# Differential scores: the keys' low-part pass on 64 rows, the two maps' passes adjacent in opposite halves of the array's rows

## The chip, the cores and the metric

The kernel runs on one core of a Trainium2 chip. The metric is the device time of one execution in microseconds, the median of several runs; lower is better.

## The reference, cut to what matters

Two layers of a decoder trunk (sequence 1024, width 1024, float32) mix tokens in three ways: differential attention, a latent attention (MLA) and a sliding window. The change touches the first alone. It has 4 heads, and each head has two maps (m) of width 64 with a common value of width 128:

```
s = einsum('bqhmd,bkhmd->bhmqk', q, k) * 64 ** -0.5      # two maps per head
s = where(rel >= 0, s + bias[head], NEG)                       # causal; bias differs in the last 256 keys only
pm = softmax(s, axis=-1)
w = pm[:, :, 0] - lam * pm[:, :, 1]
o = einsum('bhqk,bkhe->bqhe', w, v)
```

## The kernel before, in words

**Precision.** Matmuls are done in fp32r. To come close to float32, an operand x is split into a high part H, x rounded (a cast on ScalarE, line 76), and a low part L = x - H (VectorE, line 91). A projection takes three products for each tile of 128 rows: HH, HL and LH (`group`, line 294).

**Scores of the differential attention.** A map is 64 wide, half of the 128 rows of TensorE's array. `stack_q` (line 453) stacks a query tile as qH in partitions 0 to 63 and qL in 64 to 127. `stack_k` (line 464) does the same for the keys, tile kA, and two DMAs for each map and half of the sequence make a second tile kB with the halves exchanged. So q.kA = qH.kH + qL.kL and q.kB = qH.kL + qL.kH, and two passes of 128 rows give all four products. `rows` (line 629) does this for one map of one query tile of 128 rows: `n = (i + 1) * 128` causal keys, in one chunk up to 512 and two chunks beyond (`chunks`, line 623). Each chunk takes a bank of PSUM with the tag "sc" (there are two), gets its two passes (`mm`, line 99), then the bias (line 762) and the maximum (line 639) on VectorE, and after the last chunk the exponentials on ScalarE (line 645), which free the banks.

**Order.** `da` (line 697) goes through 4 heads; a head has 4 blocks (`da_block`, line 751) of two query tiles. Of a tile, map 0 is written first, then one step of the block before (`late`, its transposes and products with V) and `FILL[2]` = 2 steps of filler, then map 1, the sum of the two maps, and again a step of `late` and `FILL[1]` = 2 steps. A filler is a projection that nobody waits for yet (the gates and the units of the next head); one step is 6 matmuls of 512 columns into one of three banks with the tag "mm". The order written is a priority only: the planner of the framework issues on each engine what is ready by its own estimate, so a matmul whose bank is not free yet lets later ones pass.

**The units of a head.** `prep` (line 710) returns the units for keys, queries and values; each loads 128 columns of the input weights, splits them, and multiplies them with the 8 pairs of tiles of hT, in two halves of the sequence.

```
# rows, lines 635-640: one chunk of one map
ps = self.psum("sc")
self.mm(ps[:, :w], [(q, k[:, k0:k0 + w]) for q, k in terms])     # terms: (q, kA), (q, kB)
near(ps, k0, w)
nc.vector.tensor_reduce(st[:, c:c + 1], ps[:, :w], AX.X, ALU.max, negate=len(ch) == 1)
```

The latent attention, which the change leaves alone, has one operation on 64 rows: at line 864 it transposes the values, which lie in partitions 64 to 127, four blocks of 64 by 128 at a time.

Of the kernel before, what the change touches and what calls it, by code (L numbers as in the profile page):

```python
# [10 lines left out]
F32 = mybir.dt.float32  # L11
F32R = mybir.dt.float32r
I32 = mybir.dt.int32
AF = mybir.ActivationFunctionType
ALU = mybir.AluOpType
AX = mybir.AxisListType

P = 128
S = 1024
D = 1024  # L20
DEPTH = 2
KT = D // P
# [5 lines left out]
FILL = (3, 2, 2, 1, 1, 5, 3)  # L28
BANKS = dict(mm=3, av=1, sc=2, tr=2)
OFF = dict(aq=0, ak=512, av=1024, az=1536, bq=2048, bkv=2304, bkr=2432, bz=2464,  # L30
           cq=2976, ck=3488, cv=3616, cz=3744, g=4256)
# [27 lines left out]
class Builder:  # L59
# [404 lines left out]
    def stack_k(self, pool, l, c, tiles, swapped):  # L464
# [8 lines left out]

        yield from self.unit(W, KT, self.hT, evac)

    def v_unit(self, pool, l, c, put):
        W = self.load_w(self.win(l, c))

        def evac(hf, ps):
            vT = pool.tile([P, 512], F32, tag="vT", bufs=1, name=self.uid("vT"))  # L480
            self.copy("a", vT, ps)
            tr = self.psum("tr")
            for t in range(4):
                self.nc.tensor.transpose(tr[:, t * P:(t + 1) * P], vT[:, t * P:(t + 1) * P], self.ident)
            put(hf, tr.rearrange("p (t d) -> p t d", t=4))

        yield from self.unit(W, KT, self.hT, evac)
# [141 lines left out]
    def rows(self, pl, n, terms, near, sums):  # L629
# [16 lines left out]
                                 accum_out=sums[:, c:c + 1])  # L646
        return e

    def weighted(self, pl, ws, b, vterms):

        nc = self.nc
        terms = []
        av = self.av = self.psum("av")
        self.square_sums(av)

        def add(last):
            for i, (w, x) in enumerate(terms):
                self.nc.tensor.matmul(av[:, 0:256], w, x, start=self.first and not i,  # L658
                            stop=last and i == len(terms) - 1)
            self.first = self.first and not terms  # L660
            terms.clear()

        self.first = True
        for kp in range(b + 1):
            tr = self.psum("tr")
            if kp == b:
                self.diag.reverse()
            H, L = self.diag[0] if kp == b else self.wt_tiles(pl)

            for a in range(2):  # L670
                kt = 2 * kp + 1 - a
                for q in range(2):
                    if kt <= 2 * b + q:
                        self.nc.tensor.transpose(tr[:, (2 * a + q) * P:(2 * a + q + 1) * P],  # L674
                                       ws[q][:, kt * P:(kt + 1) * P], self.ident)
            z = P if kp == b else 0
            self.split(H[:, z:], L[:, z:], tr[:, z:])
            add(False)
            for a in (1, 0):
                kt = 2 * kp + 1 - a  # L680
                terms += vterms(kt, H[:, a * 256:(a + 1) * 256], L[:, a * 256:(a + 1) * 256])
            yield
        add(True)
# [13 lines left out]
    def da(self, l):  # L697
        nc = self.nc
        v = self.vecs[l]
        with ExitStack() as ctx:  # L700
            pl = self.pool("da", ctx)
            bias = pl.tile([P, 4, 256], F32, name=self.uid("dab"))
            nc.sync.dma_start(bias, self.bias_ap(0, 4))
            heads = []
            self.diag_tiles(pl)
            s0 = pl.tile([P, 4, 8], F32, name=self.uid("s0"))
            ms = pl.tile([P, 4, 8], F32, name=self.uid("ms"))
            self.s0, self.ms = s0, ms

            def prep(h):  # L710
                t = {}
                for nm in ("q", "kA", "kB"):
                    t[nm] = [pl.tile([P, S], F32R, tag=f"{nm}{m}", bufs=2, name=self.uid(nm))
                             for m in range(2)]
                for nm in ("VH", "VL"):
                    t[nm] = pl.tile([P, 8, P], F32R, tag=nm, bufs=2, name=self.uid(nm))

                def put(hf, tr):
                    sl = slice(hf * 4, hf * 4 + 4)
                    self.split(t["VH"][:, sl], t["VL"][:, sl], tr)  # L720

                heads.append(t)
                return (self.stack_k(pl, l, OFF["ak"] + h * P, t["kA"], t["kB"]),
                        self.stack_q(pl, l, OFF["aq"] + h * P, t["q"]),
                        self.v_unit(pl, l, OFF["av"] + h * P, put))

            for g in prep(0):
                self.weave(g, 1)
            late = iter(())
            for h in range(4):  # L730
                nxt = []
                for b in range(4):
                    late = self.da_block(l, pl, h, b, heads[h], bias, late)
                    if not b and h < 3:
                        nxt = self.later(*prep(h + 1), front=True)
                self.drain(*nxt)
            self.weave(late, FILL[1])
            self.square_sums(self.psum("av"))

            f = lambda t: t.rearrange("p h i -> p (h i)")  # L740
            s0, ms = f(s0), f(ms)
            nc.vector.reciprocal(s0, s0)
            nc.vector.tensor_tensor(ms, ms, s0, ALU.mult)
            nc.vector.tensor_tensor(ms, ms, s0, ALU.mult)
            nc.scalar.activation(ms, ms, AF.Sqrt, bias=self.eps, scale=1.0 / P)
            nc.vector.reciprocal(ms, ms)
            nc.vector.tensor_tensor(ms, ms, s0, ALU.mult)
            self.put_rows(pl, l, "a", ms)
            self.fill(FILL[6])

    def da_block(self, l, pl, h, b, t, bias, late):
        nc = self.nc
        nlam = self.vecs[l]["nlam"]
        ws = []
        for i in (2 * b, 2 * b + 1):
            n = (i + 1) * P
            es = []

            def near(ps, k0, w):
                a = max(n - 256, k0)  # L760
                if a < k0 + w:
                    nc.vector.tensor_tensor(ps[:, a - k0:w], ps[:, a - k0:w],  # L762
                                            bias[:, h, a - n + 256:k0 + w - n + 256], ALU.add)

            sm = pl.tile([P, 6], F32, tag="sm", bufs=4, name=self.uid("sm"))
            for m in range(2):
                q = t["q"][m][:, i * P:(i + 1) * P]
                es.append(self.rows(pl, n, [(q, t["kA"][m]), (q, t["kB"][m])], near,
                                    sm[:, 2 * m:2 * m + 2]))
                if not m:  # L770
                    next(late, None)
                    self.fill(FILL[2])
            e0, e1 = es
            s0 = self.s0[:, h, i:i + 1]
            if n > 512:
                nc.vector.tensor_tensor(s0, sm[:, 0:1], sm[:, 1:2], ALU.add)
                nc.vector.tensor_tensor(sm[:, 2:3], sm[:, 2:3], sm[:, 3:4], ALU.add)
            else:
                nc.gpsimd.tensor_copy(s0, sm[:, 0:1])  # L779
            nc.vector.reciprocal(sm[:, 4:5], sm[:, 2:3])  # L780
            nc.vector.scalar_tensor_tensor(sm[:, 5:6], sm[:, 4:5], nlam, s0, ALU.mult, ALU.mult)
            nc.vector.scalar_tensor_tensor(  # L782
                e0[:, :n], e1[:, :n], sm[:, 5:6], e0[:, :n], ALU.mult, ALU.add)
            ws.append(e0)
            next(late, None)
            self.fill(FILL[1])
        self.weave(late, FILL[2])

        def vterms(kt, H, L):
            return [(t["VH"][:, kt], H), (t["VH"][:, kt], L), (t["VL"][:, kt], H)]  # L790

        def rest():
            yield from self.weighted(pl, ws, b, vterms)
            o = self.zp.tile([P, 256], F32, tag="o", bufs=2, name=self.uid("o"))
            av = self.av
            self.copy("a", o, av[:, :256])
            sq = pl.tile([P, 256], F32, tag="sq", bufs=2, name=self.uid("sq"))
            nc.scalar.activation(sq, av[:, :256], AF.Square)
            self.squares = sq, self.ms[:, h, 2 * b:2 * b + 2]
            nc.sync.dma_start(self.o_d[l, "a"][h * P:(h + 1) * P, b * 256:(b + 1) * 256], o)  # L800

        return rest()
# [398 lines left out]
```

## Time and profile before

| | us |
|---|---|
| median of 3 runs (2652.02 to 2655.14) | 2653.09 |
| the profiled execution | 2655.53 |
| its span, from the first to the last instruction | 2653.8 |
| TensorE busy | 2608.1 (98%) |
| VectorE busy | 1528.0 (58%) |
| ScalarE busy | 1240.5 (47%) |
| GpSimd busy | 389.4 (15%) |

Busy time is the union of an engine's instructions. A matmul's end is modelled, and matmuls overlap, so TensorE's pace is read from one start to the next.

### The profile page before, as it was taken

Reading aid. Unit: us, or ns where it says so; the run is one execution under the profiler, and the core shown is the slowest. Engines: PE = TensorE matmul, PEld = TensorE weight load, DVE = VectorE, ACT = ScalarE, POOL = GpSimd, SP = SyncE. Lnnn points to the kernel's source line nnn. Section 1 sums busy time; section 2 is a strip of 40 time slices with the busy share of each in tenths; the row PEclk is TensorE's granted clock in tenths of the full one; section 3 lists DMA queues with packets and bytes.
Section 4 is the critical chain, followed back from the end, with each engine's and each line's share of the span. In section 5 each row is a group of like instructions: output and inputs, shape, how many; then the busy total and the mean of one; then the engine's idle time right before and its main releaser. Section 6 shows DMA issues by size and latency. Waiting matters only on the chain.

```text
span 2653.8 us, 35805 instructions
## 1 busy us (share of the span) xinstructions
PE 2608.1 (98%) x13024; PEld 2148.4 (81%) x13024; DVE 1528.0 (58%) x2928; ACT 1240.5 (47%) x2695; POOL 389.4 (15%) x359
## 2 busy tenths in 40 slices
PE   8999999999999998999999999999999999989999
PEld 6788888888888876888877788888888888778877
DVE  5664767535666445655457637664366664456653
ACT  5553545435666433333445535554266664333332
POOL 2000000000000144134410000000000001440431
PEclk9999999999999999999999999999999999999999
DMA  6223222221112576353332322222211126754432
GB/s 193 60 70 103 59 64 63 70 74 51 46 45 59 166 240 199 119 181 114 118 88 62 89 82 64 62 63 66 65 47 50 46 66 211 237 174 138 143 116 96
DMA packets 296817, 269.21 MB, mean 101 GB/s; under 512 B 24272, under 2 KB 237456, under 8 KB 296512
## 3 DMA queue, kind: packets, MB, share of 16 engines
q1 hardware_dynamic: 295568, 262.19, 32.9%
q0 software_dynamic: 1072, 4.73, 0.6%
q8 instruction: 103, 1.69, 0.3%
q14 instruction: 74, 0.61, 0.1%
HBM read 194.93 MB, written 61.44 MB: 97 GB/s over the span
## 4 chain that ended last, share of the span: by engine, by line
PE 79%; DVE 7%; DMA 4%; issue 4%; ACT 3%; POOL 2%; SPq 1%; ACTq 0%; POOLq 0%; DVEq 0%
PE mm L303 56%; PE sc L102 8%; PE av L658 5%; PE tr L674 4%; DVE wL L91 2%; PE sc L303 1%; DMA sig<-g_d 1%; ACT wH L76 1%; PE tr L595 1%; DVE sig L1014 1%; POOL y L1016 1%; DMA wr<-w_ple_proj 1%; DVE y L1018 1%; POOL o L1045 1%; ACT big L76 1%
## 5 line engine op out<-in xcount | busy, mean ns | idle before, releaser
L303 PE MATMUL mm<-big,wH 128*128 128x512 f32 x4480 | 1447.8, 396 | 1.6 <-DVE big L91 1.1
L303 PEld LDWEIGHTS mm<-big,wH 128*128 128x128 f32 x4480 | 825.3, 188 | 149.5 <-DVE big L91 1.7
L303 PE MATMUL mm<-big,wL 128*128 128x512 f32 x2240 | 882.8, 394 | 4.1 <-DVE wL L91 3.9
L303 PEld LDWEIGHTS mm<-big,wL 128*128 128x128 f32 x2240 | 421.4, 188 | 86.6 <-DVE wL L91 6.6
L91 DVE TENSOR_TENSOR wL<-wr,wH 128x1024 fp32r<-128x1024 f32 (+2 forms) x268 | 274.9, 1034 | 300.7 <-ACT wH L76 299.0
L76 ACT CAST wH<-wr 128x1024 fp32r<-128x1024 f32 (+2 forms) x268 | 229.4, 863 | 274.2 <-PE mm L303 243.3
L645 ACT ACTIVATE e<-sc,st 128x512 f32<-128x512 f32 (+3 forms) x384 | 222.5, 583 | 123.2 <-DVE st L642 69.2
L639 DVE TENSOR_REDUCE st<-sc 128x1 f32<-128x512 f32 (+3 forms) x384 | 213.0, 555 | 89.8 <-PE sc L102 83.2
L76 ACT CAST wtH<-tr 128x512 fp32r<-128x512 f32 x204 | 116.5, 588 | 100.1 <-PE tr L674 81.7
L91 DVE TENSOR_TENSOR wtL<-tr,wtH 128x512 fp32r<-128x512 f32 x204 | 139.2, 684 | 38.7 <-ACT wtH L76 37.2
L674 PE MATMUL tr<-cm,e 128*128 128x128 f32 x864 | 148.4, 274 | 0.1
L76 ACT COPY zs<-mm 128x512 f32<-128x512 f32 x144 | 84.2, 584 | 104.1 <-PE mm L303 100.1
L674 PEld LDWEIGHTS tr<-cm,e 128*128 128x128 f32 x864 | 108.2, 142 | 17.9 <-DVE e L782 2.4
L102 PE MATMUL sc<-kA,q 128*128 128x256 f32 (+3 forms) x320 | 104.5, 336 | 1.5 <-ACT e L645 0.9
L91 POOL TENSOR_TENSOR kL<-vT,kH 64x512 fp32r<-64x512 f32 x32 | 42.0, 1312 | 426.3 <-ACT kH L76 357.4
L1041 POOL TENSOR_TENSOR sg<-sg,z 128x512 f32<-128x512 f32 x48 | 71.0, 1480 | 210.5 <-ACT sg L1040 198.6
L102 PE MATMUL sc<-kB,q 128*128 128x256 f32 (+3 forms) x320 | 98.8, 318 | 0.0
L1046 DVE TENSOR_TENSOR o<-o,sg 128x512 f32<-128x512 f32 x48 | 53.7, 1129 | 71.2 <-POOL o L1045 66.7
L762 DVE TENSOR_TENSOR sc<-sc,dab 128x256 f32<-128x256 f32 (+1 forms) x128 | 52.8, 413 | 65.6 <-PE sc L102 63.7
L1007 ACT ACTIVATE sig<-sig 128x1024 f32<-128x1024 f32 x48 | 50.9, 1060 | 79.2 <-DMA sig<-g_d 79.1
L779 POOL COPY s<-sm 128x1 f32<-128x1 f32 x32 | 6.3, 196 | 528.2 <-ACT e L645 528.2
L374 POOL TENSOR_TENSOR acc<-acc,sq 128x512 f32<-128x512 f32 x36 | 57.2, 1590 | 174.6 <-ACT sq L373 67.3
(295 smaller groups left out, 4163.0 us busy)
## 6 DMA issues: line engine op xcount, KB each, us to landing
wr<-w_in SPq DMA_DIRECT2D x108, 512.0 KB, 4.0
g_d<-zs SPq DMA_DIRECT2D x96, 256.0 KB, 2.1
sig<-g_d SPq DMA_DIRECT2D x48, 512.0 KB, 3.3
wr<-w_out SPq DMA_DIRECT2D x32, 512.0 KB, 4.6
wr<-w_ple_gate SPq DMA_DIRECT2D x32, 512.0 KB, 3.7
kB<-kA SPq DMA_DIRECT2D x80, 128.0 KB, 2.4
x<-x SPq DMA_DIRECT2D x16, 512.0 KB, 6.2
wr<-w_br_a SPq DMA_DIRECT2D x8, 512.0 KB, 5.1
```

The lines of the kernel that those rows point to most:

```text
L76: nc.scalar.copy(out, in_)
L91: (nc.vector if le == "v" else nc.gpsimd).tensor_tensor(L, src, h, ALU.subtract)
L102: self.nc.tensor.matmul(ps, w, x, start=i == 0, stop=i == n - 1)
L303: self.nc.tensor.matmul(ps, w, x, start=i == 0, stop=i == n - 1)
L374: (nc.gpsimd if eng == "g" else nc.vector).tensor_tensor(st, st, sq, ALU.add)
L639: nc.vector.tensor_reduce(st[:, c:c + 1], ps[:, :w], AX.X, ALU.max, negate=len(ch) == 1)
L645: nc.scalar.activation(e[:, k0:k0 + w], pss[c][:, :w], AF.Exp, bias=st[:, 0:1], accum_out=sums[:, c:c + 1])
L658: self.nc.tensor.matmul(av[:, 0:256], w, x, start=self.first and not i, stop=last and i == len(terms) - 1)
L674: self.nc.tensor.transpose(tr[:, (2 * a + q) * P:(2 * a + q + 1) * P], ws[q][:, kt * P:(kt + 1) * P], self.ident)
L762: nc.vector.tensor_tensor(ps[:, a - k0:w], ps[:, a - k0:w], bias[:, h, a - n + 256:k0 + w - n + 256], ALU.add)
L1041: nc.gpsimd.tensor_tensor(sg, sg, z, ALU.mult)
L1046: nc.vector.tensor_tensor(o, o, sg, ALU.mult)
```

## The change

The queries of map 1 are stacked the other way round (`rows_q`): qL in partitions 0 to 63, qH in 64 to 127. The keys' tile kA (`rows_k`) now holds the high part twice, in both halves, the second by one DMA; so the first pass, q.kA, is qH.kH + qL.kH. The low parts of both maps lie in one tile kL, map 0 in partitions 0 to 63, map 1 in 64 to 127. The second pass, qH.kL, takes 64 rows: rows 0 to 63 for map 0, rows 64 to 127 for map 1. The product qL.kL is no longer computed, and kB is gone.

`two_rows` takes the place of two calls of `rows`: `two` writes, for the first chunk of a tile, the 128-row passes of both maps into the two "sc" banks and then the two 64-row passes. Biases and maxima of both maps follow. A second chunk is done map by map, its 128-row and its 64-row pass one behind the other, in an "mm" bank. The first chunk is now up to 512 keys wide and the second gets the rest, at least 256. The steps of `late` and filler stand where they stood, after map 0's exponentials. The sliding window keeps `stack_k` and `stack_q`.

```diff
--- before.py
+++ after.py
@@ -470,6 +470,31 @@
                 self.split(tiles[m][0:64, sl], tiles[m][64:128, sl], ps[m * 64:m * 64 + 64])
                 self.nc.sync.dma_start(swapped[m][0:64, sl].bitcast(F32), tiles[m][64:128, sl].bitcast(F32))
                 self.nc.sync.dma_start(swapped[m][64:128, sl].bitcast(F32), tiles[m][0:64, sl].bitcast(F32))
+
+        yield from self.unit(W, KT, self.hT, evac)
+
+    def rows_q(self, pool, l, c, tiles):
+
+        W = self.load_w(self.win(l, c))
+
+        def evac(hf, ps):
+            sl = slice(hf * 512, hf * 512 + 512)
+            for m in range(2):
+                a, b = slice(m * 64, m * 64 + 64), slice(64 - m * 64, 128 - m * 64)
+                self.split(tiles[m][a, sl], tiles[m][b, sl], ps[a], scale=0.125)
+
+        yield from self.unit(W, KT, self.hT, evac)
+
+    def rows_k(self, pool, l, c, tiles, low):
+
+        W = self.load_w(self.win(l, c))
+
+        def evac(hf, ps):
+            sl = slice(hf * 512, hf * 512 + 512)
+            for m in range(2):
+                a, b = slice(m * 64, m * 64 + 64), slice(64 - m * 64, 128 - m * 64)
+                self.split(tiles[m][a, sl], low[a, sl], ps[a])
+                self.nc.sync.dma_start(tiles[m][b, sl].bitcast(F32), tiles[m][a, sl].bitcast(F32))
 
         yield from self.unit(W, KT, self.hT, evac)
 
@@ -646,6 +671,48 @@
                                  accum_out=sums[:, c:c + 1])
         return e
 
+    def two(self, pss, qs, ks, low, at=(0, 1)):
+
+        nc = self.nc
+        for ps, q, k in zip(pss, qs, ks):
+            nc.tensor.matmul(ps, q, k, start=True, stop=False)
+        for ps, q, m in zip(pss, qs, at):
+            a = slice(m * 64, m * 64 + 64)
+            nc.tensor.matmul(ps, q[a], low[a], start=False, stop=True)
+
+    def two_rows(self, pl, n, qs, kA, kL, near, sums):
+
+        nc = self.nc
+        ch = [(0, n)]
+        if n > 512:
+            b = max(n - 512, 256)
+            ch = [(0, n - b), (n - b, b)]
+        w = ch[0][1]
+        pss = [[self.psum("sc")] for _ in range(2)]
+        sts = [pl.tile([P, 2], F32, tag="st", bufs=8, name=self.uid("st")) for _ in range(2)]
+        self.two([p[0][:, :w] for p in pss], qs, [x[:, :w] for x in kA], kL[:, :w])
+        for m in range(2):
+            near(pss[m][0], 0, w)
+            nc.vector.tensor_reduce(sts[m][:, 0:1], pss[m][0][:, :w], AX.X, ALU.max, negate=len(ch) == 1)
+        for m in range(2):
+            st = sts[m]
+            if len(ch) == 2:
+                k0, w1 = ch[1]
+                ps = self.psum("mm")
+                a = slice(m * 64, m * 64 + 64)
+                self.mm(ps[:, :w1], [(qs[m], kA[m][:, k0:n]), (qs[m][a], kL[a, k0:n])])
+                near(ps, k0, w1)
+                nc.vector.tensor_reduce(st[:, 1:2], ps[:, :w1], AX.X, ALU.max)
+                nc.vector.tensor_reduce(st[:, 0:1], st[:, 0:2], AX.X, ALU.max, negate=True)
+                pss[m].append(ps)
+            e = pl.tile([P, S], F32, tag="e", bufs=4, name=self.uid("e"))
+            for c, (k0, w) in enumerate(ch):
+                nc.scalar.activation(e[:, k0:k0 + w], pss[m][c][:, :w], AF.Exp, bias=st[:, 0:1],
+                                     accum_out=sums[m][:, c:c + 1])
+            pss[m], ps, out = None, None, [e]
+            del e
+            yield out.pop()
+
     def weighted(self, pl, ws, b, vterms):
 
         nc = self.nc
@@ -709,9 +776,10 @@
 
             def prep(h):
                 t = {}
-                for nm in ("q", "kA", "kB"):
+                for nm in ("q", "kA"):
                     t[nm] = [pl.tile([P, S], F32R, tag=f"{nm}{m}", bufs=2, name=self.uid(nm))
                              for m in range(2)]
+                t["kL"] = pl.tile([P, S], F32R, tag="kL", bufs=2, name=self.uid("kL"))
                 for nm in ("VH", "VL"):
                     t[nm] = pl.tile([P, 8, P], F32R, tag=nm, bufs=2, name=self.uid(nm))
 
@@ -720,8 +788,8 @@
                     self.split(t["VH"][:, sl], t["VL"][:, sl], tr)
 
                 heads.append(t)
-                return (self.stack_k(pl, l, OFF["ak"] + h * P, t["kA"], t["kB"]),
-                        self.stack_q(pl, l, OFF["aq"] + h * P, t["q"]),
+                return (self.rows_k(pl, l, OFF["ak"] + h * P, t["kA"], t["kL"]),
+                        self.rows_q(pl, l, OFF["aq"] + h * P, t["q"]),
                         self.v_unit(pl, l, OFF["av"] + h * P, put))
 
             for g in prep(0):
@@ -763,13 +831,13 @@
                                             bias[:, h, a - n + 256:k0 + w - n + 256], ALU.add)
 
             sm = pl.tile([P, 6], F32, tag="sm", bufs=4, name=self.uid("sm"))
-            for m in range(2):
-                q = t["q"][m][:, i * P:(i + 1) * P]
-                es.append(self.rows(pl, n, [(q, t["kA"][m]), (q, t["kB"][m])], near,
-                                    sm[:, 2 * m:2 * m + 2]))
-                if not m:
-                    next(late, None)
-                    self.fill(FILL[2])
+            two = self.two_rows(pl, n, [x[:, i * P:(i + 1) * P] for x in t["q"]], t["kA"], t["kL"],
+                                near, [sm[:, 0:2], sm[:, 2:4]])
+            es.append(next(two))
+            next(late, None)
+            self.fill(FILL[2])
+            es.append(next(two))
+            two.close()
             e0, e1 = es
             s0 = self.s0[:, h, i:i + 1]
             if n > 512:
```

## Rows read from the trace of the kernel before

**Rows 1.** The page, engines over the span, and TensorE's granted clock in 40 slices.

```profile
PE 2608.1 (98%) x13024; PEld 2148.4 (81%) x13024; DVE 1528.0 (58%) x2928; ACT 1240.5 (47%) x2695; POOL 389.4 (15%) x359
...
PEclk9999999999999999999999999999999999999999
```

**Rows 2.** Busy time by stage: PE, PEld, DVE, ACT, POOL, clock, DMA share, GB/s.

```profile
252.00:507.00 255.00, 254.47 (x1343) 211.85 (x1343) 175.24 (x409) 126.58 (x317) 3.14 (x16) 1.00 0.24 66
```

**Rows 3.** What PE waited for from 252 to 507 us: total, times, longest.

```profile
PE sc L102 <- ACT e L645: 0.5, 2, 0.2
```

**Rows 4.** Timeline of PE: start, us, engine, line, operation, tiles, shapes, count.

```profile
256.24 0.28 PE L102 MATMUL sc<-kA,q 128*128 128x256 f32 x1
256.35 0.28 PE L102 MATMUL sc<-kB,q 128*128 128x256 f32 x1
256.47 0.40 PE L303 MATMUL mm<-big,wH 128*128 128x512 f32 x1
...
501.92 0.39 PE L102 MATMUL sc<-kA,q 128*128 128x512 f32 x1
502.15 0.39 PE L102 MATMUL sc<-kB,q 128*128 128x512 f32 x1
502.37 0.40 PE L303 MATMUL mm<-big,wH 128*128 128x512 f32 x1
502.60 0.39 PE L102 MATMUL sc<-kA,q 128*128 128x512 f32 x1
```

**Rows 5.** Line 102 from 252 to 507 us: count, ns min/median/max, first and last, shapes.

```profile
L102 PE MATMUL sc<-kA,q x95: 220/387/501, 254.6 to 506.4; 128*128 128x512 f32 x40, 128*128 128x256 f32 x24, 128*128 128x384 f32 x24, 128*128 128x128 f32 x7
```

**Rows 6.** Timeline around a group of 64-row transposes (L864), PE and its weight loads.

```profile
619.42 0.61 PE L303 MATMUL mm<-big,wH 128*128 128x512 f32 x2
...
619.88 0.19 PEld L303 LDWEIGHTS mm<-big,wH 128*128 128x128 f32 x1
620.10 0.39 PE L303 MATMUL mm<-big,wH 128*128 128x512 f32 x1
...
620.42 0.33 PEld L864 LDWEIGHTS tr<-cm,vT 64*128 64x128 f32 x4 [0.35 <-ACT vT L76]
620.42 0.46 PE L864 MATMUL tr<-cm,vT 64*128 64x64 f32 x4
620.81 0.19 PEld L303 LDWEIGHTS mm<-big,wH 128*128 128x128 f32 x1
620.81 0.50 PE L303 MATMUL mm<-big,wH 128*128 128x512 f32 x1
...
621.15 0.39 PE L303 MATMUL mm<-big,wL 128*128 128x512 f32 x1
```

**Rows 7.** Line 864, the 64-row transposes, whole span: count, ns min/median/max, shapes.

```profile
L864 PE MATMUL tr<-cm,vT x128: 221/223/273, 620.4 to 2161.5; 64*128 64x64 f32 x128
```

**Rows 8.** Timeline of PE around another group, between matmuls of 256 columns.

```profile
649.45 0.28 PE L658 MATMUL av<-wtH,vp 128*128 128x256 f32 x1
649.57 0.28 PE L658 MATMUL av<-wtL,vp 128*128 128x256 f32 x1
649.78 0.46 PE L864 MATMUL tr<-cm,vT 64*128 64x64 f32 x4
650.17 0.38 PE L658 MATMUL av<-wd,vp 128*128 128x256 f32 x1
```

**Rows 9.** Timeline of PE around four 128-row transposes.

```profile
882.23 0.39 PE L303 MATMUL mm<-big,wL 128*128 128x512 f32 x1
882.46 0.60 PE L674 MATMUL tr<-cm,e 128*128 128x128 f32 x4
882.81 0.71 PE L303 MATMUL mm<-big,wH 128*128 128x512 f32 x2
```

**Rows 10.** Instructions of tile kA, whole span: a cast and one swap DMA.

```profile
L76 ACT CAST kA<-mm x40: 571/582/586, 27.1 to 1733.2; 64x512 fp32r<-64x512 f32 x40
...
L471 SPq DMA_DIRECT2D kB<-kA x40: 461/462/1058, 32.8 to 1734.7; - x40
```

**Rows 11.** The page, groups by line: busy us, mean ns of one, idle before.

```profile
L645 ACT ACTIVATE e<-sc,st 128x512 f32<-128x512 f32 (+3 forms) x384 | 222.5, 583 | 123.2 <-DVE st L642 69.2
L639 DVE TENSOR_REDUCE st<-sc 128x1 f32<-128x512 f32 (+3 forms) x384 | 213.0, 555 | 89.8 <-PE sc L102 83.2
...
L674 PE MATMUL tr<-cm,e 128*128 128x128 f32 x864 | 148.4, 274 | 0.1
```

## The prediction

> **What bounds the kernel now.** I read the page first. TensorE is busy 98% of the span, VectorE 58%, ScalarE 47%, at a granted clock of nine tenths or more in all forty slices [rows 1]. Busy matmul time is modelled and overlaps, so I went on to the stage that is changed, the differential attention, which runs once in each of the two layers. In the first layer's, 255 us from 252 to 507 us, TensorE is busy 254.5 us and VectorE 175 [rows 2]. The waits of TensorE in it add up to 0.5 us, on ScalarE's exponentials that give score banks back [rows 3]. So nothing but TensorE's own instruction stream sets the length of this stage, because projection matmuls ("fillers") are put between the scores wherever they would wait. What the change does to the stream arrives in the total one to one; what it does to VectorE, ScalarE or the DMA queues hardly arrives at all.
>
> The stream is read from start to start. Scores of 512 columns follow each other, and other matmuls, every 0.227 us (501.92, 502.15, 502.37), 256 columns every 0.115 (256.24, 256.35, 256.47) [rows 4]; for 384 and 128 columns I take the same rate, 0.17 and 0.06. At that pace the weight loads cost nothing: each load starts about when the matmul ahead of its own starts, and is done before its own matmul (the load at 619.88 serves the matmul at 620.10) [rows 6].
>
> **Part 1, the number of matmuls and their columns: nothing.** Before, each chunk of each map is two passes of 128 rows. After, it is again two, the second on 64 rows. The first stretch has 95 records of the first pass [rows 5]; by the loops it is 4 heads x (4 tiles with one chunk + 4 with two, 12 chunks) x 2 maps = 96, and as many of the second. Columns per pass decide a matmul's time, and they stay; that half of the rows is idle shortens nothing by itself. The chunk order changes (384+256, 512+256 and 512+384 for 256+384, 256+512 and 384+512), the sums are the same.
>
> **Part 2, the two low passes side by side.** The gain can only come where the two 64-row passes run at once. That is one pair for each tile: per head the first chunks have 128, 256, 384, 512, 384, 512, 512 and 512 columns, and there are 4 heads x 2 layers = 8 such heads, so 64 pairs. If the second pass starts c after the first instead of a full pass later, a head saves the passes' own time, 0.06 + 0.115 + 2 x 0.17 + 4 x 0.227 = 1.42 us, less 8c. In the only 64-row work of this trace, loads and matmuls of that size step every 0.06 us (below), so I take c = 0.06: 0.94 us a head, 7.5 us in all. The bounds are c = 0 (11.4 us) and c = a full pass (nothing).
>
> **Part 3, going from 128 rows to 64 and back.** Before, the scores never leave 128 rows. The trace shows a stretch of 64 rows in one place: the latent attention's transposes of line 864, 32 groups of four [rows 7]. Around the one at 620.42 us [rows 6]: three matmuls go at (620.10 - 619.42)/3 = 0.227 us, then the first transpose starts 0.32 after the last of them, 0.09 late. Its load does not start ahead of it, as all loads before did, but together with it, and the first transpose lasts 0.273 (the longest) where the median is 0.223 [rows 7]: 0.05 of load is laid bare. The four then step by (0.46 - 0.22 - 0.05)/3 = 0.06. Back on 128 rows the same again: load and matmul both start at 620.81, the matmul is marked 0.50 instead of 0.39, and the next follows after 0.34, not 0.23. From 620.10 to 621.15 are 1.05 us; two matmuls of 0.227 and four transposes of 0.06 are 0.70; 0.35 us remain for going in and out. At 649.78, between matmuls of 256 columns, the same: 0.21 instead of 0.12 on the way in, and on the way out a matmul marked 0.38 for 0.28 [rows 8]. The control is a group of four 128-row transposes among the same matmuls. They begin at the usual step (882.23, 882.46) and step by (0.60 - 0.27)/3 = 0.11 [rows 9, 11], so they are through at 882.90; the two matmuls behind them end at 883.52, which is 0.61, their usual time for two [rows 6], behind 882.91. Going in and out cost 0.01. So the price hangs on the number of rows, not on transposing.
>
> Of this 0.35, some 0.14 is the way in (0.09 + 0.05) and 0.20 the way out. The way in may hold a wait, since the profile books the idle time to a ScalarE copy [rows 6]; the way out has no such excuse. Bounds for one visit to 64 rows: nothing, if score matmuls are treated otherwise than these transposes; 0.20 if only the way out counts; 0.35 as the rows have it, which I take, as it is the only measured stretch of this kind; 0.40 if a bare load for scores is as long as the 0.11 of the way out. The Trainium skill (TensorEngine Tiling (Array Packing), Key Properties) says that a change of the tiling mode, unlike a mere change of tile, drains TensorE. By that rule every visit pays, as the rows have it; without it the sum would be that of part 2 alone.
>
> The visits: 64 pairs, and as many more for the second chunks, since there each map runs its own 64-row pass right behind its own 128-row pass, with nothing beside it: 8 heads x 4 tiles x 2 maps = 64. So 128 visits x 0.35 = 44.8 us, of which part 2 gives back 7.5: **37 us longer**.
>
> **Part 4, who stands between the two low passes.** The written order is high, high, low, low. But the planner already lets other matmuls in where a bank is not free: between the two chunks of one map stands a projection at 502.37 [rows 4]. A tile's pair now wants both score banks at once, and the second comes free only when the other map's exponential is done: the bias, a maximum of 0.56 and an exponential of 0.58 us [rows 11]. With 12 filler matmuls (2.7 us) between, this is mostly over. Where it is not, the first map's low pass goes alone, and the pair is two visits: 0.35 + about 0.15 more. I put a quarter of the 32 two-chunk pairs there: 8 x 0.5 = 4 us. Bounds: none, and all 64 pairs, 22 + 7.5 = 30 us.
>
> **Part 5, what else moves, at nothing.** Of the 80 swap DMAs 64 belong to this stage (40 at line 471 [rows 10] and as many at line 472; 16 evacuations of 4 here); 32 remain, on SP's queue, and the DMA engines are busy a quarter of the time [rows 2]. The copy that is left needs only the high half, and is issued one split earlier. The splits keep their count and shape (0.58 us each on ScalarE) [rows 10], only halves are swapped. Second chunks sit in the projections' three banks for about 2 us, and the fillers fill one bank at a time. If that cover failed, the projections would wait on a bank some tenths of a microsecond for each of 64 chunks, under 10 us. Dropping the product of the two low parts removes no instruction.
>
> **Sum.** The profiled execution took 2655.5 us (span 2653.8), 2.4 over the median of the runs, 2653.1. 37 + 4 = 41 us on it is 2696.6; on the median, **2694 us**, which I predict (1.5% slower).
>
> **Rivals.**
> - *The visits are cheap and the pairs run together: faster.* Decides when one visit costs less than (11.4 or 7.5)/128 = 0.09 or 0.06 us. At no price at all it is 2653 - 11.4 or - 7.5 = 2642 or 2646 us. For it: the trace holds no 64-row matmul of scores, and the first half of the rows was never used alone. Against: the way out is paid in both groups read here. The Trainium skill (TensorE: Matmul & The Clock Gate, The mechanism) has matmuls in different row groups start about 4 ns apart; that is the lower end of c, and by itself this rival. Chance 0.10.
> - *Half price: the way in is hidden by the queue, the way out is paid.* 128 x 0.20 - 7.5 = 18 us, with the split pairs about 20: 2671 to 2674 us. Chance 0.16.
> - *It does not do what it says: the two low passes run one after the other.* 128 x 0.35 + 4 = 49 us: 2702 us. I count this with the forecast, 2684 to 2712; together 0.64.
> - *The pairs are mostly split, or a step from one half to the other costs a visit of its own.* 37 + 30, or 37 + 64 x 0.35 = 59 to 67 us: 2712 to 2720 us. Chance 0.06.
> - *The gains and costs cancel*, near 0.08 us a visit: 2648 to 2658 us, chance 0.04.
>
> **How the numbers follow.** A measurement of this kernel tells 0.2% (5.3 us) from no change. Slower by more: 0.64 + 0.16 + 0.06 = 0.86; within: 0.04; faster: 0.10. The range takes the forecast's own 2684 to 2712 and the half price below it: 2662 to 2712, which leaves out 0.20.
>
> **What would show it.** In the changed stages, the 64-row score matmuls begin together with their weight load, not after it, and so does the first 128-row matmul behind them; the stages grow from 255 to about 275 us each, all of TensorE's other stretches staying as they are. Part 2 is right if the second low pass starts 0.06 us after the first, wrong if 0.2. Part 4 is right if few pairs have a projection between them. If the steps in and out are as long as between 128-row matmuls, the price was that of transposes alone and the forecast fails, on the fast side.

## The result and the profile after

The changed kernel takes 2689.63 us (median of 4 runs, 2686.85 to 2690.29) against 2654.11 us before in the same session: a ratio of 1.0132, 95% interval 1.0114 to 1.0149. It is 35.5 us slower; 2694 was forecast.

The engines over the span, from the page after, to be set beside [rows 1]: TensorE's busy time grows by 35.5 us, about what the span grows (33.5), with the same number of matmuls; no other engine's grows by more than 1.6.

```profile
span 2687.3 us, 35707 instructions
PE 2643.6 (98%) x13024; PEld 2145.7 (80%) x13024; DVE 1517.2 (56%) x2928; ACT 1238.3 (46%) x2695; POOL 391.0 (15%) x359
PEclk9999999999999998999999999999999999999999
```

Where it went, by landmarks of both traces (first and last bias of the differential attention, first projection of the latent attention, its merge): the bias stretch grows from 254.98 to 269.42 us in the first layer and from 254.86 to 269.41 in the second, the tail behind it from 27.4 to 31.3 in both. That is 18.3 us a layer, 36.6 in all. The profiled spans differ by only 33.5: from the first projection of the latent attention to the second layer's first bias the profile after is 4.4 us shorter (1033.8 to 1029.3 us), and behind the second layer's tail it is 1.4 us longer. TensorE's stops there fall differently in the two profiles. Before, it waits 2.9 us for a split at 952 us, its matmuls behind that are marked 0.77 instead of 0.39, and the mean granted clock from 945 to 975 us is 0.94, so for a part of it the lower level (1.2 GHz) was granted; after, it stops at 1013 us, and the mean from 1005 to 1030 us is 0.93.

Timeline of TensorE and of its weight loads around a pair of 512 columns, in the trace after. Count, start and length are read as in [rows 6]:

```profile
268.15 0.39 PE L303 MATMUL mm<-big,wL 128*128 128x512 f32 x1
268.38 0.61 PE L678 MATMUL sc<-kA,q 128*128 128x512 f32 x2
268.92 0.50 PE L681 MATMUL sc<-kL,q 64*128 64x512 f32 x2
269.35 0.73 PE L303 MATMUL mm<-big,wH 128*128 128x512 f32 x2
269.92 0.40 PE L303 MATMUL mm<-big,wL 128*128 128x512 f32 x1
...
268.15 0.41 PEld L678 LDWEIGHTS sc<-kA,q 128*128 128x128 f32 x2
268.92 0.19 PEld L681 LDWEIGHTS sc<-kL,q 64*128 64x128 f32 x2 [0.35 <-issue]
269.35 0.30 PEld L303 LDWEIGHTS mm<-big,wH 128*128 128x128 f32 x2 [0.25 <-issue]
```

The two low passes run together: both lie within 0.50 us, and the records put the second 0.003 us behind the first. The two high passes are 0.61 for two, as filler is. But the low passes start with their loads, not behind them (268.92 both), 0.32 after the second high pass instead of 0.23; and the first filler behind them again starts with its load (269.35), 0.43 after, and its pair is marked 0.73 instead of 0.61. From the start of the second high pass (268.38 + 0.23 = 268.61) to that of the second filler (0.73 - 0.39 = 0.34 behind 269.35, 269.69) are 1.08 us. Three full passes of 0.227 are 0.68; 0.40 is the price of the visit, for which 0.227 of overlap was bought.

A second chunk, one map alone, has the price without the purchase. 256 columns take 0.115 from start to start on 128 rows [rows 4]; here the low pass follows its high pass after 0.32, and what follows it comes after 0.31. About 0.1 of the 0.32 is still the price of the pair in front, since this high pass too starts with its load (last row):

```profile
274.01 0.45 PE L681 MATMUL sc<-kL,q 64*128 64x384 f32 x2
274.38 0.38 PE L102 MATMUL mm<-kA,q 128*128 128x256 f32 x1
274.70 0.38 PE L102 MATMUL mm<-kL,q 64*128 64x256 f32 x1
275.01 0.61 PE L759 MATMUL av<-ones,sq 128*128 128x1 f32 x4
...
274.38 0.19 PEld L102 LDWEIGHTS mm<-kA,q 128*128 128x128 f32 x1 [0.19 <-issue]
```

The loads of those low passes, one line from 250 to 530 us (count, ns minimum/median/maximum): with 64 rows they take 0.183, nearly what 128-row loads take (0.187), where those of the 64-row transposes took 0.134 to 0.142. The last two rows, from the trace of before, show that the shorter load belongs to the transposes and not to the 64 rows: on 128 rows theirs takes 0.140.

```profile
L102 PEld LDWEIGHTS mm<-kA,q x32: 186/187/192, 274.4 to 518.9; 128*128 128x128 f32 x32
L102 PEld LDWEIGHTS mm<-kL,q x32: 182/183/183, 274.7 to 519.5; 64*128 64x128 f32 x32
...
L864 PEld LDWEIGHTS tr<-cm,vT x128: 134/138/142, 620.4 to 2161.5; 64*128 64x128 f32 x128
L674 PEld LDWEIGHTS tr<-cm,e x864: 137/140/226, 264.1 to 2205.1; 128*128 128x128 f32 x173
```

Who held the load queue, before (first line; 252 to 507 us) and after (the rest; 252 to 521 us): total us, times, longest. "issue" is idle time with nothing in the profile to wait for.

```profile
PEld sc L102 <- ACT e L645: 6.0, 24, 0.7
```

```profile
PEld mm L102 <- issue: 9.5, 38, 0.4
PEld sc L681 <- issue: 9.2, 32, 0.4
...
PEld sc L678 <- ACT e L710: 1.6, 3, 0.6
```

The idle time "issue" stands at the low passes and at what follows them (15 of the 38 are high passes behind a pair): no semaphore, only the change of rows. The bank waits of before have mostly gone.

**The ledger of a stage.** For every matmul from the first bias to the latent attention I took the step to the next start, less the usual step for its columns (0.227, 0.172, 0.115 and 0.057 for 512, 384, 256 and 128; 0.109 between 128-row transposes, 0.028 behind the last). The excess, in us for the first layer (the second agrees within 0.15 in each line):

| | before | after |
|---|---|---|
| into 64 rows (71 visits) | | 8.7 |
| out of 64 rows | | 14.4 |
| next step behind that | | 4.8 |
| second low pass beside the first (25 pairs) | | -4.4 |
| 128-row scores, into, within and behind | 5.9 | 1.9 |
| all else | 8.8 | 7.7 |
| sum | 14.7 | 33.1 |

So 71 visits cost 27.8 us, 0.39 each. There are 142 in two layers: 64 second chunks, 50 pairs, and 14 pairs that the planner split in two.

### The profile page after: what moved, and what is told of

The parts are those of the page before. It is cut to its first block, busy times and chain, and to the rows that moved or that the text cites. A ratio compares the mean times of both kernels' runs of the same rounds, so it can differ in the third digit from the quotient of the medians.

```text
span 2687.3 us, 35707 instructions
## 1 busy us (share of the span) xinstructions
PE 2643.6 (98%) x13024; PEld 2145.7 (80%) x13024; DVE 1517.2 (56%) x2928; ACT 1238.3 (46%) x2695; POOL 391.0 (15%) x359
## 4 chain that ended last, share of the span: by engine, by line
PE 84%; DMA 4%; DVE 4%; issue 3%; ACT 2%; POOL 2%; SPq 1%; ACTq 0%; POOLq 0%; DVEq 0%
PE mm L303 57%; PE sc L102 6%; PE av L725 5%; PE tr L741 4%; PE sc L303 3%; PE tr L303 2%; PE mm L102 1%; DMA sig<-g_d 1%; PE sc L681 1%; DVE wL L91 1%; PE tr L620 1%; PE sc L678 1%; DMA z<-z_d1a 1%; DVE o L1114 1%; POOL o L1113 1%
## 5 line engine op out<-in xcount | busy, mean ns | idle before, releaser
L664 DVE TENSOR_REDUCE st<-sc 128x1 f32<-128x128 f32 (+2 forms) x192 | 106.7, 556 | 47.9 <-PE sc L102 44.9
L710 ACT ACTIVATE e<-sc,st 128x512 f32<-128x512 f32 (+3 forms) x128 | 76.0, 595 | 107.1 <-DVE st L706 48.2
L670 ACT ACTIVATE e<-sc,st 128x128 f32<-128x128 f32 (+2 forms) x192 | 111.4, 583 | 16.5 <-DVE st L664 10.7
L696 DVE TENSOR_REDUCE st<-sc 128x1 f32<-128x512 f32 (+3 forms) x128 | 69.7, 567 | 16.1 <-PE sc L681 12.5
L76 ACT CAST wd<-tr 128x384 fp32r<-128x384 f32 x96 | 46.0, 479 | 67.2 <-PE tr L741 67.2
```

The costliest lines, as they stand in the source:

```text
L76: nc.scalar.copy(out, in_)
L670: nc.scalar.activation(e[:, k0:k0 + w], pss[c][:, :w], AF.Exp, bias=st[:, 0:1], accum_out=sums[:, c:c + 1])
L696: nc.vector.tensor_reduce(sts[m][:, 0:1], pss[m][0][:, :w], AX.X, ALU.max, negate=len(ch) == 1)
L710: nc.scalar.activation(e[:, k0:k0 + w], pss[m][c][:, :w], AF.Exp, bias=st[:, 0:1], accum_out=sums[m][:, c:c + 1])
```

## The experiments

The diffs are cut to the lines that matter. The first four were run together (before: 2652.5 us in that session), then three (2653.8), then four (2652.7). Ratios are to the kernel before, with the 95% interval.

**1. The low pass on 128 rows.** Each map gets its own kL tile with zeros in the other half; all else is as in the changed kernel.

```diff
-            nc.tensor.matmul(ps, q[a], low[a], start=False, stop=True)
+            nc.tensor.matmul(ps, q, low[m], start=False, stop=True)
-                self.mm(ps[:, :w1], [(qs[m], kA[m][:, k0:n]), (qs[m][a], kL[a, k0:n])])
+                self.mm(ps[:, :w1], [(qs[m], kA[m][:, k0:n]), (qs[m], kL[m][:, k0:n])])
```

> As the changed kernel in order, banks, chunks and copies, but the low pass runs on 128 rows: each map has its own tile of low parts whose other half is zero, so no matmul of the scores leaves 128 rows. Theory (each visit to 64 rows costs about 0.39 us in the changed kernel's trace, 142 visits, and 50 pairs that overlap give back 8.7 us): 2689.6 - 55.7 + 8.7 = 2643, and up to 8 us more where loads behind a bank wait are laid bare on 128 rows as they were before, so 2643 to 2652 us, within 0.4% of the kernel before. Rival (the new order, both banks wanted at once and second chunks in the projections' banks are what costs): it stays at 2680 us or more.

Measured: 2651.86 us, 0.9998 (0.9989 to 1.0008). The whole loss is gone, with the order, the banks, the chunks and the halved copies of the changed kernel still in place. The rival is out. The stage is back at 251.8 us from first to last bias. Its tail is 31.1 us, as in the changed kernel, so the longer tail belongs to the new order and not to the visits; together they are 283.0 us, against 282.4 before.

**2. Only the pairs on 64 rows.** The same tiles; first chunks as in the changed kernel, second chunks on 128 rows.

```diff
-            nc.tensor.matmul(ps, q, low[m], start=False, stop=True)
+            nc.tensor.matmul(ps, q[a], low[m][a], start=False, stop=True)
```

> First chunks keep their 64-row low passes, second chunks' low passes run on 128 rows against tiles with a zero half. TensorE's order is that of the changed kernel. That leaves 78 of 142 visits. Theory: 2689.6 - 64 x 0.39 = 2665 us, up to 4 more for loads laid bare by bank waits: 2664 to 2669 us. Rival (the pairs' order and banks cost, not the visits): no less than 2680 us.

Measured: 2668.24 us, 1.0062 (1.004 to 1.0084). As expected: with 64 rows only where the passes mostly overlap, they still lose. The planner split 18 of the 64 pairs here, not 14, so its trace has 46 overlapping pairs and 82 visits, not the 78 expected.

**3. Both low passes in the same half.**

```diff
-        self.two([p[0][:, :w] for p in pss], qs, [x[:, :w] for x in kA], kL[:, :w])
+        self.two([p[0][:, :w] for p in pss], qs, [x[:, :w] for x in kA], kL[:, :w], at=(0, 0))
```

> The first chunks' low pass of map 1 uses rows 0 to 63 as map 0's does (it multiplies the other operands' halves, so map 1's scores lack their proper low part). Same instructions, same order. Theory (the two passes overlap because they lie in different rows): the second low pass now starts a full pass after the first, 0.23 us at 512 columns instead of 0.003, and 50 pairs lose 8.7 us: 2698 us. Rival (they overlap because they go to different banks, or the start stamps say nothing): within 2 us of 2690.

Measured: 2696.06 us, 1.0157 (1.0139 to 1.0174); its profiled span is 8.2 us over that of the changed kernel. The pair at the same place in its trace takes 0.73 for two, not 0.50, and the next matmul comes 0.66 after it, not 0.43:

```profile
268.82 0.61 PE L678 MATMUL sc<-kA,q 128*128 128x512 f32 x2
269.37 0.73 PE L681 MATMUL sc<-kL,q 64*128 64x512 f32 x2
270.03 0.73 PE L303 MATMUL mm<-big,wH 128*128 128x512 f32 x2
```

So the overlap is real, and comes from the opposite halves. The time to the next matmul grows by 0.23, one pass. (The intervals of the two ratios, 1.0132 and 1.0157, still overlap; it is the rows that show it.)

**4. The order of before with the changed tiles.** `da_block` calls `rows` again, map by map.

```diff
-            es.append(next(two))
+                es.append(self.rows(pl, n, [(q, t["kA"][m]), (q[a], t["kL"][a, :])], near,
+                                    sm[:, 2 * m:2 * m + 2]))
```

> The tiles of the changed kernel, but the scores in the order, chunks and banks of the kernel before: per map and chunk a 128-row pass and behind it a 64-row pass, never two together. 192 visits and no overlap. Theory (price per visit): 2689.6 + 50 x 0.39 + 8.7 = 2718 us. Rival (price per 64-row matmul, of which there are 192 in both): only the overlap is lost, 2698 us. Rival (order and banks cost in the changed kernel): less than 2690 us.

Measured: 2718.89 us, 1.0245 (1.0225 to 1.0265). The price is one per visit, not one per 64-row matmul: 192 such matmuls run in both kernels, in 142 visits there and 192 here.

The four with the result give one price. With experiment 1 as the kernel without visits, the extra time plus the overlap won, divided by the visits: (35.5 + 8.7)/142 = 0.31 for the changed kernel, (17.0 + 7.8)/82 = 0.30 in 2, 42.2/142 = 0.30 in 3, 65.5/192 = 0.34 in 4 (ratios less 0.9998, times 2653; the intervals leave 0.03 to 0.07 either way). It lies under the ledger's 0.39 because 128-row scores lose time at bank waits too, laying their loads bare: in the ledger of experiment 1 the 128-row scores stand at 5.5 us and "all else" at 9.5, together 5.4 more than in the changed kernel, or 0.08 for each of its 71 visits.

**5. Fewer visits: does it pay then?** If a visit costs 0.3 to 0.4 and a pair of 512 wins 0.23, two pairs in one visit should break even. Seven kernels tried it. First, the pairs pinned in the order written, so that none is split:

```diff
-            nc.tensor.matmul(ps, q, k, start=True, stop=False)
+            self.keep(nc.tensor.matmul(ps, q, k, start=True, stop=False))
-            nc.tensor.matmul(ps, q[a], low[a], start=False, stop=True)
+            self.keep(nc.tensor.matmul(ps, q[a], low[a], start=False, stop=True))
```

> The changed kernel with TensorE's first-chunk passes pinned in the order written (high, high, low, low), so that no pair is split: 128 visits to 64 rows for 142, and 64 overlapping pairs for 50. Theory: 14 x 0.40 = 5.6 us of visits and 14 x about 0.2 = 2.8 us of overlap are gained: 2681 us (2679 to 2684). Rival (waiting for the second bank costs what the split cost): 2688 to 2692 us.

Then all 128-row passes of a tile in four banks (two "sc", two "mm"), and all its 64-row passes behind them, pinned too:

```diff
+        for c, (k0, w1) in enumerate(ch):
+            for m in range(2):
+                self.keep(nc.tensor.matmul(pss[m][c][:, :w1], qs[m], kA[m][:, k0:k0 + w1], start=True, stop=False))
+        for c, (k0, w1) in enumerate(ch):
+            for m in range(2):
+                a = slice(m * 64, m * 64 + 64)
+                self.keep(nc.tensor.matmul(pss[m][c][:, :w1], qs[m][a], kL[a, k0:k0 + w1], start=False, stop=True))
```

> All 128-row passes of a tile (both maps, both chunks) first, in four banks, then all its 64-row passes, in pinned order: 64 visits, and second chunks overlap too. Against the kernel with low passes on 128 rows (2651.9): 64 x 0.40 = 25.6 us for visits, less 16.4 us of overlap (2.05 us for each of 8 heads), less 4 to 8 us of loads that 128-row scores lay bare behind bank waits: 2653 to 2657 us. Rival (a visit costs more the more matmuls are in it, or four banks at once starve the projections): 2665 us or more.

And the same for tiles with two chunks alone, the others as in experiment 1 (the second pass is `(qs[m], kL[m])` where there is one chunk):

> Tiles with one chunk do their low pass on 128 rows against a tile with a zero half, tiles with two chunks make one visit for all four low passes: 32 visits. Theory: against 2651.9, 32 x 0.40 = 12.8 us for visits, less 11.9 us of overlap, less 2 to 4 us of loads no longer laid bare: 2649 to 2652 us, the same as before. Rival (four banks at once starve the projections): 2656 us or more.

Measured: 2696.69 us, 1.0159 (1.0142 to 1.0176); 2690.83 us, 1.0145 (1.013 to 1.016); 2688.7 us, 1.0135 (1.012 to 1.015). All three theories fell: 14, 78 and 110 visits were saved, and the time did not fall; the pinned pairs came out above their rival's range as well. The longest waits of TensorE in the kernel with one visit a tile, 252 to 523 us, say who took a part of it; [rows 3] has 0.5 us of waits in the same stage.

```profile
PE mm L303 <- ACT e L716: 6.6, 4, 2.0
PE mm L303 <- DVE q L93: 2.0, 3, 1.1
PE mm L303 <- DVE kL L91: 1.9, 2, 0.9
PE mm L698 <- ACT e L716: 1.6, 3, 0.5
```

The projections wait for the exponentials that give "mm" banks back, and for VectorE's splits, which also empty them. In the ledger the visits with their overlap cost 5.6 us a layer here (23.5 in the changed kernel), but the line "all else" went from 7.7 to 26.4.

The waits are not all of that. The first two rows below are the stage in the changed kernel and in this one (columns as in [rows 2]): the mean granted clock falls from 1.00 to 0.97. Behind four of the longer waits TensorE ran at the lower level (1.2 GHz) for a while, as in the other two rows, where 512 columns step by 0.43 instead of 0.227.

```profile
252.00:523.00 271.00, 269.88 (x1332) 208.37 (x1333) 172.66 (x410) 125.84 (x318) 2.94 (x16) 1.00 0.19 54
252.00:523.00 271.00, 258.41 (x1326) 207.66 (x1325) 169.20 (x408) 122.66 (x311) 2.96 (x16) 0.97 0.19 53
...
356.53 0.63 PE L303 MATMUL mm<-big,wL 128*128 128x512 f32 x1
356.96 1.05 PE L303 MATMUL mm<-big,wH 128*128 128x512 f32 x2
```

By the ledger's steps the lower clock took about 6 of the 18.7 us. All seven kernels of this group have such stretches in the changed stages, one to four a layer; the changed kernel and experiment 1 have none.

Two causes of the waits were open: the pins, which also keep a high pass and the projections from passing each other, or the banks. So the pin was loosened to one (low passes not before the last high pass), or dropped. The four kernels, in the order of their expectations: the pairs with the one pin (the edit shown), one visit a tile without a pin, the same with the one pin, and the one pin with the visit for tiles of two chunks alone.

```diff
+            ins = nc.tensor.matmul(ps, q[a], low[a], start=False, stop=True)
+            if i == 0:
+                self.keep(ins)
```

> The changed kernel with one pin alone: a first chunk's low passes may not go before both its high passes have been issued; all else floats as in the changed kernel. 128 visits and 64 overlapping pairs, as in the kernel with the pairs kept. Theory A (that kernel lost because its pins kept the high passes and the projections from passing each other): 14 visits and 2.8 us of overlap are gained, 2679 to 2684 us. Theory B (holding map 0's low pass back for the second bank costs what the visit saves, since its bias, maximum and exponential start later and the banks come free later): 2688 to 2697 us.

> As the kernel with one visit a tile, but nothing is pinned, so the planner may let projections through: 84 visits, 80 overlapping pairs. Theory A (pins starved the projections there): 2689.6 - 58 x 0.40 - 4.5 = 2662 us, and up to 4 more. Theory B (it was the four banks that a tile takes from scores and projections together): 2675 us or more, with waits of projections on exponentials in the trace.

> One visit a tile, with one pin: a tile's first low pass not before its last high pass. 78 visits, 92 overlapping pairs. Theory A (pins on the high passes starved the projections): 2689.6 - 64 x 0.40 - 6 = 2658 us, and up to 4 more. Theory B (four banks): 2675 us or more.

> Short tiles' low passes on 128 rows, long tiles' four low passes on 64 rows with the one pin. About 50 visits. Theory A: 2650 to 2656 us. Theory B (four banks): 2668 us or more.

Measured: 2690.14 us, 1.0139 (1.0122 to 1.0156); 2692.58 us, 1.0148 (1.0133 to 1.0163); 2689.9 us, 1.0138 (1.0121 to 1.0154); 2686.16 us, 1.0125 (1.0108 to 1.0143). The times are those of theory B four times; that the banks alone are the cause is not shown. With the one pin on the pairs, the visits with their overlap cost 1.8 us a layer less in the ledger than in the changed kernel, and as much came back elsewhere: TensorE's waits on exponentials grew from 1.0 us (first row) to 3.4, and behind the longest of them, 1.1 us, the lower clock was granted for a while, another 1.6 us. In the unpinned kernel (last three rows) no projection waits for an exponential, which was theory B's sign; the scores do, and the projections wait for VectorE's splits of keys and queries.

```profile
PE sc L678 <- ACT e L710: 1.0, 3, 0.4
...
PE sc L678 <- ACT e L712: 2.5, 3, 1.1
PE mm L303 <- ACT e L712: 0.7, 2, 0.3
...
PE sc L698 <- ACT e L716: 3.6, 3, 1.4
PE mm L303 <- DVE kL L91: 2.6, 2, 1.3
PE mm L303 <- DVE q L93: 2.0, 3, 1.0
```

In the third of the four, TensorE is busy 257.9 of 269 us, against 254.5 of 255 in [rows 2]:

```profile
252.00:521.00 269.00, 257.91 (x1326) 205.76 (x1324) 170.69 (x407) 123.69 (x312) 2.94 (x16) 0.99 0.19 53
```

Which share of these waits is due to the banks taken and which to low passes held back was not separated; a kernel with more banks for scores was not tried, since all eight are given out.

## Why the prediction was right, step by step

The time and the cause were as forecast; the sum was nearer than its terms. The signs came as listed: low passes, and the 128-row matmuls behind them, begin with their loads, and the stage grew to 269.4 us, with 3.9 more in its tail, where about 275 was expected.

- *Part 1* held: 13024 matmuls in both, and the usual steps unchanged.
- *Part 2*, the overlap, held, with c = 0.003 where 0.06 was taken: 50 pairs win 8.7 us by the ledger, 7.5 was forecast for 64. The lower bound was the right one.
- *Part 3*, the step that decides, held in kind: in and out are paid at each visit, and experiment 1 takes all of it away. Its size was 0.39 us by the ledger, not 0.35. The mis-sized term is the bare load on the way in. I took the transposes' 0.05, but a transpose's load is shorter on 128 rows as well (shown above); score loads on 64 rows last as long as 128-row loads, and the visit at 268.92 needs 0.40, which was the upper bound. 142 visits came to 55.7 us; 136 x 0.35 = 47.6 had been put down.
- *Part 4*: 14 pairs were split, not 8. That a split is a loss, as I argued, was not borne out: the kernel that forbids it (the one pin) is no faster. There the wait for the second bank, which the planner's projection between the two low passes would cover, is paid as a wait (2.5 us for score banks, not 1.0) and in the lower clock behind it.
- *Part 5* was wrong in one point that I had at nothing. The bank waits of the scores of before [rows 3] looked like 0.5 us, but they hold the weight loads, 6.0 us of idle time in the load queue (shown above), and 5.9 us a layer in the ledger. In the changed kernel 1.9 remain. That is 8.0 us less in two layers, and "all else" is 2.2 less. It does not come from the second chunks' other banks: experiment 1 has the same banks and order, and 5.5 in that line. It goes with the visits, whether because a low pass behind its high pass pays its load as part of the visit or because a longer stream waits less for banks; which of the two was not separated.
- *The sum*: 55.7 - 8.7 - 8.0 - 2.2 = 36.8 against 41 forecast. An under-priced visit (8.1 us) and an overlooked credit (10.2) cancelled for the most part. That the sum came so near is to that extent luck; the kind of the cost is not.
- *The rivals.* That the visits are cheap is refuted by experiments 1 and 2, that the low passes run one after the other by the trace and experiment 3. "Half price" missed the measured time by 16 us, but the net price of 0.31 a visit lies nearer to the full one. A step from one half to the other costs nothing (0.003 us). Nor were the pairs mostly split (14 of 64), nor did gains and costs cancel.
- *The rule of the Trainium skill* that a change of tiling mode drains TensorE (TensorEngine Tiling (Array Packing), Key Properties) agrees with this trace: 0.09 us late on the way in and again on the way out, with the loads starting only then. Its companion that a mere change of tile does not is borne out by the 0.003 us between the halves.

## What to carry to other kernels

Price a new shape of matmul by the place where the old trace already has it, and by both ends: look whether the weight load starts ahead of its matmul or with it. Half-array passes that overlap win one pass, but each excursion among 128-row matmuls cost 0.3 to 0.4 us here, more than the 0.227 us that a pair of 512 columns won; they would have to stay together by twos at least, and every kernel tried here that kept them together lost as much to TensorE's waits, and to the lower clock granted behind them. Adding zero rows to keep the array's full height cost nothing.

## What the runs showed that was not expected

- The loads of two opposite halves go side by side as well: a visit with two loads and two matmuls of 512 columns is 0.43 us from its start to the next (268.92 to 269.35), and one with a single load and matmul is 0.43 as well (the records' median).
- Within 64 rows in the same half, loads are hidden again: experiment 3 adds one pass of 0.23 us, and no load.
- A wait of some tenths of a microsecond for a bank costs more than it shows at the matmuls, since the load queue waits too and the load is laid bare: 0.5 us of waits in [rows 3] stood beside 5.9 us of excess.
- Kernels with fewer visits traded them for waits, and the waits cost twice: once as idle time, and again where the granted clock fell behind them (1.00 to 0.97 in the stage with one visit a tile, some 6 us of it).
